# A hybrid decoder block: the recurrence's output projection put ahead of the convolution's

## The chip, the cores and the metric

The kernel runs on one core of a Trainium2 chip, in float32. The metric is the device time of one execution in microseconds (us), as the median of several runs. Three runs of the kernel before gave 1181.91, 1185.55 and 1191.15 us. The engines are named as the profile names them: PE is TensorE's matrix multiply and PEld its weight load, DVE is VectorE, ACT is ScalarE, POOL is GpSimd, SP is SyncE, which here only issues transfers; ACTq and SPq are the queues of two engines.

## The reference

512 tokens of width 1024, with 16 learned tokens ahead of them, go through one layer. What matters here is the mixing half:

```python
p = h @ w_in[l]                                   # one input projection, columns cut into parts
y_conv = conformer_conv(p[..., :c_end], ...)      # GLU, 31-tap conv, LayerNorm over channels, silu, @ w_conv_out
y_rwkv = rwkv7_time_mix(p[..., c_end:r_end], ...) # recurrence over time, norm per head, gate, @ w_rwkv_out
gates = jax.nn.sigmoid(p[..., r_end:] + b_gate[l])
y = gates[..., :D_MODEL] * y_conv + gates[..., D_MODEL:] * y_rwkv
h = layer_norm(ALPHA * h + y @ w_o[l], ln1_g[l], ln1_b[l])
h = layer_norm(ALPHA * h + conv_gated_mlp(h, ffn_up[l], ffn_dw[l], ffn_down[l]), ln2_g[l], ln2_b[l])
```

## The kernel before, in words

Activations lie channels first: 128 channels on the partitions, 514 or 528 tokens along a row, eight such blocks for the width of 1024. Float32 products are made of three passes: every operand is split into a high and a low part (`split`, L136: ACT casts the high part, L138, DVE subtracts it for the low one, L141), and `gemm` (L158) multiplies high by high, low by high and high by low, so that one block of 128 outputs costs two halves of 258 and 256 columns with 8 x 3 matmuls each: 48 in all. `wload` (L155) brings a block of weights from memory (SP, 512 KB), splits it, and holds it in two buffers of each kind, which all products share in turn; so the products follow each other in the order in which the code asks for their weights. Their results go to three PSUM banks (`gbank`).

The code is a long list of steps that SCHEDULE (L50) puts in order. A compiler turns it into one instruction stream for each engine: it takes the steps' place in the list as a priority, and gives an engine that is free the first instruction that is ready. `front()` raises the priority of some of them (weight loads, PSUM reads). A tile whose space is used again waits for the readers of the tile that lay there.

The steps, for block p of eight (two heads of the recurrence each):

- G: the convolution's GLU; T or the second number of S: the convolution, run on DVE between the dependent instructions of a solve; its result is stored to `c_dr` (L725).
- K: three projections; P (`prep`, L347): decays, keys, and the blocks `Gt` of a triangular system.
- S (`solve`, L482): the system's inverse, 31 dependent steps on DVE (L520 to L526, tile `W`), after a trip of `Gt` through memory (`dA`, `L`).
- C (`merge`, L548, and `chain`, L581): the inverse comes back, and nine chunks of the recurrence run one after the other on PE (L584), ACT and DVE.
- F (`finish`, L624): the norm per head, the gate, and a store to `o_dr` (L673).
- A (`gate`, L728): one of 16 blocks of the branch gates, a product from `hhi`, `hlo` with tanh, stored to `g_dr`. A gate depends on nothing but its weights.
- N (`conv_norm`, L745): the eight blocks `c_t` come back from `c_dr`, are normalised over the channels and split into `zh`, `zl`.

After the list come, each over eight blocks: the convolution's projection (L811, operands `zh`, `zl`; result times its gate to `ya_dr`); the loads of `o_dr` into `o_t` with two buffers and their split into `oh`, `ol` (L832); the recurrence's projection (L838; result times its gate, plus `ya`, split into `yh`, `yl`); then the mixing product with `w_o` and the LayerNorm, in two halves of the tokens (L860 to L896), where the first NKEEP blocks of `w_o` are kept in split form for the second half and the others are loaded twice. The feed-forward part follows.

Pools of memory are opened and closed by hand: `scan` (steps S, C, F, A) on the left, `proj` (steps G, K, P, convolution) on the right, later `conv` in the place of `proj`, and `rout` in the place of `scan`. The text says product z for the convolution's projection, product o for the recurrence's, product y for the mixing one, and pair 7 for the last pair of heads with its steps S7, C7 and F7.

Of the kernel before, what the change touches and what calls it, by code (L numbers as in the profile page):

```python
# [42 lines left out]
GN_EPS = 64e-5  # L43
EXPM05 = float(np.exp(-0.5))
BACK = 3000
NKEEP = 6
GW = 132


SCHEDULE = ("G0 K0 P0 T0 G1 S01 K1 P1 C0 K2 F0 G2 S12 K3 P2 C1 G3 F1 K4 S23 G4 P3 C2 F2 A S34 K5 P4 C3 F3 G5 S4 A "  # L50
            "T5 K6 P5 G6 C4 F4 S56 P6 C5 K7 F5 G7 S67 A A A P7 C6 F6 S7 A A C7 A A N A A A A A A A F7")


@with_exitstack
def hybrid_block(ctx: ExitStack, tc: tile.TileContext, a, out, dbg=None):
# [730 lines left out]
    for step in SCHEDULE.split():  # L786
        what, p, q = step[0], int(step[1:2] or 0), int(step[2:] or -1)
        if what == "K":
            raw[p] = rkv(p)
        elif what == "P":  # L790
            prs[p] = prep(p, *raw.pop(p))
        elif what == "S":
            solved[p] = solve(prs[p], conv(q, cpads.pop(q)) if q >= 0 else ())
        elif what == "C":
            with front():
                merge(prs[p], *solved[p])
                ys[p] = chain(prs[p])
        elif what == "F":
            finish(prs[p], ys.pop(p))
        elif what == "G":  # L800
            cpads[p] = glu(p)
        elif what == "T":
            with back():
                for _ in conv(p, cpads.pop(p)):
                    pass
        elif what == "A":
            gate(gates.pop(0))
        elif what == "N":
            ctx_a1.close()
            rb, zh, zl = conv_norm()  # L810
    for j in range(NK):  # L811
        ga = rb.tile([P, NQ], F32, name="ga", bufs=2)
        nc.sync.dma_start(out=ga, in_=g_dr[j])
        w = wload(a["w_conv_out"][0], P * j)
        for sl, n in qsl:
            pt = gbank()
            gemm(pt[:, :n], w, lambda k, s: zh[k][:, s], lambda k, s: zl[k][:, s], sl)
            with front():
                V.scalar_tensor_tensor(out=ga[:, sl], in0=ga[:, sl], scalar=1.0, in1=pt[:, :n],
                                       op0=ALU.add, op1=ALU.mult)  # L820
        nc.sync.dma_start(out=ya_dr[j], in_=ga)
    ctx_b1.close()
    ctx_a2.close()


    ctx_b2, ctx_o = ExitStack(), ExitStack()
    op = pool(ctx_o, "rout", "left")
    mp = pool(ctx_b2, "mix", "right")
    ot = lambda dt, name: op.tile([P, NQ], dt, name=name, tag="ot", bufs=16)
    yt = lambda dt, name: mp.tile([P, NQ], dt, name=name, tag="yt", bufs=16)  # L830
    oh, ol, yh, yl = [], [], [], []
    for j in range(NK):  # L832
        o_t = op.tile([P, NQ], F32, name="o_t", bufs=2)
        nc.sync.dma_start(out=o_t, in_=o_dr[j])
        oh.append(ot(F32R, "oh"))
        ol.append(ot(F32R, "ol"))
        split(oh[j], ol[j], o_t)
    for j in range(NK):  # L838
        gb_ = op.tile([P, NQ], F32, name="gb_", bufs=2)
        nc.sync.dma_start(out=gb_, in_=g_dr[8 + j])  # L840
        ya = op.tile([P, NQ], F32, name="ya", bufs=2)
        nc.sync.dma_start(out=ya, in_=ya_dr[j])
        w = wload(a["w_rwkv_out"][0], P * j)
        yh.append(yt(F32R, "yh"))
        yl.append(yt(F32R, "yl"))
        for sl, n in qsl:
            pt = gbank()
            gemm(pt[:, :n], w, lambda k, s: oh[k][:, s], lambda k, s: ol[k][:, s], sl)
            with front():
                V.scalar_tensor_tensor(out=gb_[:, sl], in0=gb_[:, sl], scalar=1.0, in1=pt[:, :n],  # L850
                                       op0=ALU.add, op1=ALU.mult)
            V.tensor_tensor(out=ya[:, sl], in0=ya[:, sl], in1=gb_[:, sl], op=ALU.add)
            S.activation(out=yh[j][:, sl], in_=ya[:, sl], func=AF.Copy, scale=0.5)
            V.scalar_tensor_tensor(out=yl[j][:, sl], in0=ya[:, sl], scalar=0.5, in1=yh[j][:, sl].bitcast(F32),
                                   op0=ALU.mult, op1=ALU.subtract)


    ctx_o.close()
    h1h, h1l = hhi[:, :, Q0:T], hlo[:, :, Q0:T]
    ctx_f = ExitStack()  # L860
    fw = pool(ctx_f, "upw", "left")
    kept = [wload(a["w_o"][0], P * j, mp, bufs=NKEEP) for j in range(NKEEP)]
    half_tile = lambda name, n, bufs: mp.tile([P, 258], F32, name=name, bufs=bufs)[:, :n]
    for (t0, t1), (sl, n) in zip(QH, qsl):
        pm, pv = abank(), abank()
        xs = []
        s1, s2 = half_tile("s1", n, 1), half_tile("s2", n, 1)
        for j in range(NK):
            w = kept[j] if j < NKEEP else wload(a["w_o"][0], P * j)
            pt = gbank()  # L870
            gemm(pt[:, :n], w, lambda k, s: yh[k][:, s], lambda k, s: yl[k][:, s], sl)
            x1 = half_tile("x1", n, 10)
            with front():
                V.scalar_tensor_tensor(out=x1, in0=hlo[:, j, t0:t1].bitcast(F32), scalar=ALPHA,
                                       in1=pt[:, :n], op0=ALU.mult, op1=ALU.add)
                V.scalar_tensor_tensor(out=x1, in0=hhi[:, j, t0:t1].bitcast(F32), scalar=ALPHA,
                                       in1=x1, op0=ALU.mult, op1=ALU.add)
            xs.append(x1)
            if j > 0:
                V.tensor_tensor(out=s1, in0=xs[0] if j == 1 else s1, in1=x1, op=ALU.add)  # L880
        TE.matmul(pm[:, :n], ones_d, s1, start=True, stop=True)
        with front():
            for j in range(NK):
                V.tensor_tensor(out=xs[j], in0=xs[j], in1=pm[:, :n], op=ALU.subtract)
                sq = s2 if j == 0 else half_tile("xsq", n, 2)
# [4 lines left out]
            rs1 = mp.tile([P, 258], F32, name="rs1")[:, :n]  # L890
            S.activation(out=rs1, in_=pv[:, :n], func=AF.Sqrt, bias=eps_ln)
            V.reciprocal(out=rs1, in_=rs1)
            for j in range(NK):
                V.tensor_tensor(out=xs[j], in0=xs[j], in1=rs1, op=ALU.mult)
                S.activation(out=xs[j], in_=xs[j], func=AF.Identity, scale=par("ln1_g", j), bias=par("ln1_b", j))
                split(h1h[:, j, sl], h1l[:, j, sl], xs[j], "s")  # L896
    dump("h1", h1h.bitcast(F32))


    fl = ExitStack()  # L900
    ctx_b2.close()
    fp = pool(fl, "ffn", "right")
    hidh = fp.tile([P, NF, SEQ], F32R, name="hidh")
# [113 lines left out]
```

## Time and profile before

| | us |
|---|---|
| median of three runs | 1185.55 |
| lowest, highest | 1181.91, 1191.15 |
| the profiled execution, own time | 1188.6 |
| its span in the trace | 1186.6 |
| PE busy in it | 1128.4 (95%) |
| DVE busy in it | 870.5 (73%) |
| ACT busy in it | 560.5 (47%) |

The profile is of one execution. Times in its views count from the span's start. A matmul's busy time is longer than its share of the stream, since matmuls are pipelined; where a rate is wanted, the count of matmuls in a stretch is divided by the stretch. A few matmul records are missing. The granted clock is given as a share of full speed, 2.4 GHz; its lower level, 1.2 GHz, shows as 0.5.

### The profile page before, as it was taken

Reading aid. Unit: us, or ns where it says so; the run is one execution under the profiler, and the core shown is the slowest. Engines: PE = TensorE matmul, PEld = TensorE weight load, DVE = VectorE, ACT = ScalarE, POOL = GpSimd, SP = SyncE. Lnnn points to the kernel's source line nnn. Section 1 sums busy time; section 2 is a strip of 40 time slices with the busy share of each in tenths; the row PEclk is TensorE's granted clock in tenths of the full one; section 3 lists DMA queues with packets and bytes.
Section 4 is the critical chain, followed back from the end, with each engine's and each line's share of the span. In section 5 each row is a group of like instructions: output and inputs, shape, how many; then the busy total and the mean of one; then the engine's idle time right before and its main releaser. Section 6 shows DMA issues by size and latency. Waiting matters only on the chain.

```text
span 1186.6 us, 22669 instructions
## 1 busy us (share of the span) xinstructions
PE 1128.4 (95%) x8718; PEld 1062.5 (90%) x8718; DVE 870.5 (73%) x2195; ACT 560.5 (47%) x1195; POOL 85.0 (7%) x242
## 2 busy tenths in 40 slices
PE   4998999999999999999978989999999999999997
PEld 3997989989898989998978989989999999998885
DVE  8598988989899998986495346688876666652227
ACT  3544355647556565666575433346433443432120
POOL 6001011101101110101000000000000000000000
PEclk9999999999999999999898989999999999999999
DMA  5324241333424143344443376523332323343321
GB/s 159 82 80 106 64 117 41 90 82 89 95 60 108 41 104 84 79 121 108 135 125 85 103 209 193 164 58 85 107 100 80 104 75 107 90 134 98 93 85 71
DMA packets 202439, 118.99 MB, mean 100 GB/s; under 512 B 50036, under 2 KB 186397, under 8 KB 202331
## 3 DMA queue, kind: packets, MB, share of 16 engines
q1 hardware_dynamic: 182992, 113.81, 34.1%
q10 hardware_dynamic: 17515, 3.17, 1.5%
q8 instruction: 68, 1.11, 0.4%
q0 software_dynamic: 1824, 0.57, 0.2%
q14 instruction: 40, 0.33, 0.1%
HBM read 102.24 MB, written 15.28 MB: 99 GB/s over the span
## 4 chain that ended last, share of the span: by engine, by line
PE 60%; DVE 8%; DMA 7%; ACT 3%; issue 2%; ACTq 0%; SPq 0%; DVEq 0%; POOL 0%; POOLq 0%
PE ps_g L161 13%; PE ps_g L162 13%; PE ps_g L163 13%; PE ps_x L584 7%; PE psf L961 3%; PE psf L963 3%; PE psf L962 3%; DMA wr<-in_w_o_dram 2%; DMA t22s<-dT 1%; DMA o_t<-o_dr 1%; DVE wl L141 1%; ACT wh L138 1%; PE ps_a L450 1%; DMA wr<-in_ffn_up_dram 1%; PE ps_m L571 1%
## 5 line engine op out<-in xcount | busy, mean ns | idle before, releaser
L161 PE MATMUL ps_g<-hhi,wh 128*128 128x256 f32 (+2 forms) x1648 | 477.2, 290 | 7.9 <-ACT hf_t L277 3.9
L162 PE MATMUL ps_g<-hhi,wl 128*128 128x256 f32 (+2 forms) x1648 | 477.3, 290 | 0.0
L163 PE MATMUL ps_g<-hlo,wh 128*128 128x256 f32 (+2 forms) x1648 | 474.6, 289 | 0.0
L161 PEld LDWEIGHTS ps_g<-hhi,wh 128*128 128x128 f32 x1648 | 312.8, 190 | 11.3 <-ACT hf_t L277 4.5
L162 PEld LDWEIGHTS ps_g<-hhi,wl 128*128 128x128 f32 x1648 | 312.4, 190 | 2.6 <-issue 0.6
L163 PEld LDWEIGHTS ps_g<-hlo,wh 128*128 128x128 f32 x1648 | 312.9, 190 | 1.3 <-issue 0.4
L141 DVE TENSOR_TENSOR wl<-wr,wh 128x1024 fp32r<-128x1024 f32 x151 | 184.1, 1220 | 96.6 <-ACT wh L138 96.0
L138 ACT CAST wh<-wr 128x1024 fp32r<-128x1024 f32 x151 | 158.0, 1047 | 124.8 <-PE psf L962 75.2
L722 DVE SCALAR_TENSOR_TENSOR cev<-cd,drv,cev 128x257 f32<-128x257 f32 x216 | 99.1, 478 | 0.1
L919 ACT COPY pu<-ps_g 128x258 f32<-128x258 f32 (+1 forms) x88 | 32.8, 373 | 111.1 <-PE ps_g L163 111.0
L584 PE MATMUL ps_x<-UV,Gt 128*66 128x64 f32 (+1 forms) x576 | 71.3, 246 | 4.2 <-DMA Gt<-dT 3.8
L584 PEld LDWEIGHTS ps_x<-UV,Gt 128*66 128x66 f32 (+1 forms) x576 | 65.5, 168 | 6.1 <-DMA Gt<-dT 4.0
L961 PE MATMUL psf<-wh,hidh 128*128 128x512 f32 x176 | 69.3, 394 | 0.0
L963 PE MATMUL psf<-wl,hidh 128*128 128x512 f32 x176 | 69.0, 392 | 0.0
L962 PE MATMUL psf<-wh,hidl 128*128 128x512 f32 x176 | 68.3, 388 | 0.0
L926 DVE SCALAR_TENSOR_TENSOR u<-pu,prm,u 128x512 f32<-128x512 f32 x88 | 65.7, 748 | 1.3
L714 DVE SCALAR_TENSOR_TENSOR csh<-cpad,drv,csh 128x257 f32<-128x257 f32 x120 | 57.5, 479 | 0.5
L615 DVE SCALAR_TENSOR_TENSOR Sb<-Sb,lc,ps_x 64x64 f32<-64x64 f32 x112 | 31.3, 280 | 32.7 <-PE ps_x L584 31.2
L924 DVE TENSOR_SCALAR u<-pu,prm 128x512 f32<-128x512 f32 x44 | 21.2, 485 | 43.5 <-ACT pu L919 43.4
L524 DVE TENSOR_TENSOR stmp<-L,W 128x60 f32<-128x60 f32 (+21 forms) x216 | 45.3, 210 | 1.3
L526 DVE TENSOR_TENSOR W<-W,stmp 128x60 f32<-128x60 f32 (+21 forms) x216 | 45.2, 209 | 1.0
L161 PE MATMUL ps_g<-zh,wh 128*128 128x258 f32 (+1 forms) x128 | 38.5, 303 | 7.6 <-ACT zh L138 7.6
(308 smaller groups left out, 1991.9 us busy)
## 6 DMA issues: line engine op xcount, KB each, us to landing
wr<-in_w_in_dram SPq DMA_DIRECT2D x59, 512.0 KB, 4.3
wr<-in_ffn_up_dram SPq DMA_DIRECT2D x44, 512.0 KB, 4.0
wr<-in_ffn_down_dram SPq DMA_DIRECT2D x22, 512.0 KB, 3.7
wr<-in_w_o_dram SPq DMA_DIRECT2D x10, 512.0 KB, 4.9
g_dr<-gt SPq DMA_DIRECT2D x16, 257.0 KB, 3.0
L<-dA SPq DMA_DIRECT2D x32, 128.0 KB, 4.2
wr<-in_w_conv_out_dram SPq DMA_DIRECT2D x8, 512.0 KB, 4.4
wr<-in_w_rwkv_out_dram SPq DMA_DIRECT2D x8, 512.0 KB, 5.6
```

Of the source, the lines that this page charges most:

```text
L138: S.copy(out=dst_hi, in_=src)
L141: V.tensor_tensor(out=dst_lo, in0=src, in1=dst_hi.bitcast(F32), op=ALU.subtract)
L161: TE.matmul(ps, wh[:, k, :], xh(k, sl), start=(k == 0), stop=False)
L162: TE.matmul(ps, wl[:, k, :], xh(k, sl), start=False, stop=False)
L163: TE.matmul(ps, wh[:, k, :], xl(k, sl), start=False, stop=(k == nk - 1))
L584: mm = lambda o, l, r, start: TE.matmul(o, l, r, start=start, stop=True, skip_group_check=True)
L714: yield V.scalar_tensor_tensor(out=cs_, in0=x1[:, i:i + NM], scalar=dcol(D_SCW, 8 * i + j) if i < HT else dcol(D_HCW, 8 * 2 * i + j), in1= ...
L722: yield V.scalar_tensor_tensor(out=yp[:, b, :] if lasttap else ev[:, b, :], in0=d[:, i:i + NM], scalar=dcol(D_HCW, 8 * (2 * i + b) + j), i ...
L926: V.scalar_tensor_tensor(out=u, in0=p_[:, t:t + SEQ], scalar=pcol(C_FW, 44 * t + m), in1=u, op0=ALU.mult, op1=ALU.add)
L961: TE.matmul(acc[t][d], hidh[:, k, ts], wd[k][0][:, ds], start=(k == 0), stop=False)
L962: TE.matmul(acc[t][d], hidl[:, k, ts], wd[k][0][:, ds], start=False, stop=False)
L963: TE.matmul(acc[t][d], hidh[:, k, ts], wd[k][1][:, ds], start=False, stop=(k == NF - 1))
```

## The change

Four edits. First, the order after the list: the loads and splits of `o_t` and product o come first, `conv_norm` and product z second. What product o gives, times its gate, is stored to `ya_dr` and read back in product z, where the sum, the factor 0.5 and the split into `yh`, `yl` now are. Step N leaves the list. Second, `o_t` has eight buffers instead of two. Third, the list: one gate moves from ahead of P7 and three now stand behind F7; with the others, ten gates stand behind C7 and N is gone. Fourth, NKEEP is 4 instead of 6. Pools move with this: the mixing tiles lie on the left, in the place of `rout`, and the LayerNorm's tiles have a pool of their own, `norm1`, on the right.

```diff
-NKEEP = 6
+NKEEP = 4
-            "T5 K6 P5 G6 C4 F4 S56 P6 C5 K7 F5 G7 S67 A A A P7 C6 F6 S7 A A C7 A A N A A A A A A A F7")
+            "T5 K6 P5 G6 C4 F4 S56 P6 C5 K7 F5 G7 S67 A A P7 C6 F6 S7 A A C7 A A A A A A A F7 A A A")
...
-        elif what == "N":
-            ctx_a1.close()
-            rb, zh, zl = conv_norm()
+
+    ctx_a2.close()
+    ctx_o = ExitStack()
+    op = pool(ctx_o, "rout", "left")
...
     for j in range(NK):
-        ga = rb.tile([P, NQ], F32, name="ga", bufs=2)
+        o_t = op.tile([P, NQ], F32, name="o_t", bufs=NK)
+        nc.sync.dma_start(out=o_t, in_=o_dr[j])
+        oh.append(ot(F32R, "oh"))
+        ol.append(ot(F32R, "ol"))
+        split(oh[j], ol[j], o_t)
+    for j in range(NK):
+        gb_ = op.tile([P, NQ], F32, name="gb_", bufs=2)
+        nc.sync.dma_start(out=gb_, in_=g_dr[8 + j])
+        w = wload(a["w_rwkv_out"][0], P * j)
+        for sl, n in qsl:
+            pt = gbank()
+            gemm(pt[:, :n], w, lambda k, s: oh[k][:, s], lambda k, s: ol[k][:, s], sl)
+            with front():
+                V.scalar_tensor_tensor(out=gb_[:, sl], in0=gb_[:, sl], scalar=1.0, in1=pt[:, :n],
+                                       op0=ALU.add, op1=ALU.mult)
+        nc.sync.dma_start(out=ya_dr[j], in_=gb_)
+    ctx_a1.close()
+    rb, zh, zl = conv_norm()
+    ctx_o.close()
+    ctx_f, ctx_b2 = ExitStack(), ExitStack()
+    fw = pool(ctx_f, "upw", "left")
+    mp = pool(ctx_b2, "mix", "left")
...
+    for j in range(NK):
+        ga = mp.tile([P, NQ], F32, name="ga", bufs=2)
         nc.sync.dma_start(out=ga, in_=g_dr[j])
+        ya = mp.tile([P, NQ], F32, name="ya", bufs=2)
+        nc.sync.dma_start(out=ya, in_=ya_dr[j])
         w = wload(a["w_conv_out"][0], P * j)
+        yh.append(yt(F32R, "yh"))
+        yl.append(yt(F32R, "yl"))
...
-        nc.sync.dma_start(out=ya_dr[j], in_=ga)
-    ctx_b1.close()
-    ctx_a2.close()
...
-        o_t = op.tile([P, NQ], F32, name="o_t", bufs=2)
...
-            V.tensor_tensor(out=ya[:, sl], in0=ya[:, sl], in1=gb_[:, sl], op=ALU.add)
+            V.tensor_tensor(out=ya[:, sl], in0=ya[:, sl], in1=ga[:, sl], op=ALU.add)
...
+    ctx_b1.close()
...
+    ctx_n = ExitStack()
+    lnp = pool(ctx_n, "norm1", "right")
     kept = [wload(a["w_o"][0], P * j, mp, bufs=NKEEP) for j in range(NKEEP)]
-    half_tile = lambda name, n, bufs: mp.tile([P, 258], F32, name=name, bufs=bufs)[:, :n]
+    half_tile = lambda name, n, bufs: lnp.tile([P, 258], F32, name=name, bufs=bufs)[:, :n]
...
+    ctx_n.close()
     ctx_b2.close()
```

## Rows read from the trace of the kernel before

**Rows 1.** Windows: stretch, length, busy PE, PEld, DVE, ACT, POOL (instructions), clock, DMA, GB/s.
```profile
614.64:638.16 23.52, 12.90 (x73) 11.95 (x73) 19.42 (x48) 15.10 (x23) 0.29 (x1) 0.71 0.21 50
638.16:693.73 55.57, 55.57 (x470) 53.35 (x470) 23.05 (x55) 22.53 (x53) 0.00 (x0) 1.00 0.51 157
693.73:707.29 13.56, 10.15 (x56) 9.08 (x54) 4.51 (x8) 3.98 (x7) 0.00 (x0) 0.75 0.71 197
707.29:747.42 40.13, 40.09 (x330) 39.88 (x331) 27.08 (x52) 14.88 (x24) 0.00 (x0) 1.00 0.58 171
747.42:799.52 52.10, 48.66 (x392) 47.49 (x391) 42.80 (x92) 20.67 (x37) 0.00 (x0) 1.00 0.35 102
```

**Rows 2.** Waits of PE, 540 to 820 us: line, for whom, total, times, longest.
```profile
PE ps_g L161 <- ACT zh L138: 7.6, 1, 7.6
PE ps_g L161 <- ACT oh L138: 2.9, 3, 1.5
```

**Rows 3.** Timeline of PE: C6's end, last gate matmul, C7's first and last chunk.
```profile
593.66 0.66 PE L584 MATMUL ps_x<-UV,Gt 128*128 128x64 f32 x4
...
614.36 0.28 PE L163 MATMUL ps_g<-hlo,wh 128*128 128x256 f32 x1
...
642.25 0.40 PE L584 MATMUL ps_x<-UV,Gt 128*66 128x64 f32 x4
...
666.43 0.64 PE L584 MATMUL ps_x<-UV,Gt 128*128 128x64 f32 x4
```

**Rows 4.** Timeline of SP: transfers issued, with time and the issue's length.
```profile
569.22 0.45 SPq L752 DMA_DIRECT2D c_t<-c_dr  x1
570.49 1.24 SPq L502 DMA_DIRECT2D L<-dA  x3
580.50 0.40 SPq L147 DMA_DIRECT2D wr<-in_w_in_dram  x1
580.94 0.58 SPq L502 DMA_DIRECT2D L<-dA  x1
...
677.75 0.38 SPq L673 DMA_DIRECT2D o_dr<-on  x1
...
680.99 0.90 SPq L834 DMA_DIRECT2D o_t<-o_dr  x2
```

**Rows 5.** Timeline of DVE: S7's first and last steps.
```profile
588.45 0.82 DVE L520 SCALAR_TENSOR_TENSOR W<-L,W 128x31 f32<-128x31 f32 x3
...
630.96 0.17 DVE L526 TENSOR_TENSOR W<-W,stmp 128x8 f32<-128x8 f32 x1
```

**Rows 6.** Windows of two tiles (length, DVE busy): first `c_t` with ACT, then `W` with POOL.
```profile
588.45:631.13 42.68, 19.87 (x36) 11.74 (x19) 0.87 0.34 107
...
588.45:631.13 42.68, 12.59 (x58) 0.00 (x0) 0.87 0.34 107
```

**Rows 7.** Groups of DVE instructions in that stretch: busy us, mean ns, idle before.
```profile
L141 DVE TENSOR_TENSOR wl<-wr,wh 128x1024 fp32r<-128x1024 f32 x4 | 4.9, 1218 | 0.0
L769 DVE TENSOR_TENSOR qsum<-qsum,csq 128x514 f32<-128x514 f32 x7 | 4.8, 690 | 0.0
...
L774 DVE RECIPROCAL rstd<-rstd 128x258 f32<-128x258 f32 (+1 forms) x2 | 3.5, 1749 | 0.0
```

**Rows 8.** Timeline of ACT: the first casts of `o_t`.
```profile
686.31 1.33 ACT L138 CAST oh<-o_t 128x514 fp32r<-128x514 f32 x2 [2.81 <-DMA o_t<-o_dr]
```

**Rows 9.** Chain that ended last, pieces of C6: start, length, what.
```profile
570.63 1.17 PE ps_x L584 x6
...
574.37 0.73 PE ps_x L584 x6
...
577.52 0.70 PE ps_x L584 x6
```

**Rows 10.** Windows, columns as in rows 1: a stretch of C6, one of product o.
```profile
566.00:574.00 8.00, 8.00 (x54) 7.55 (x53) 4.62 (x18) 3.86 (x13) 0.00 (x0) 0.63 0.47 107
698.00:706.00 8.00, 6.53 (x34) 6.35 (x33) 2.08 (x3) 1.24 (x2) 0.00 (x0) 0.57 0.86 245
```

**Rows 11.** Transfers: what, queue, count, size, median us from issue to landing.
```profile
o_dr<-on SPq DMA_DIRECT2D x8, 257.0 KB, 3.0
...
o_t<-o_dr SPq DMA_DIRECT2D x8, 257.0 KB, 5.1
```

More of the change, by code (lines that the diff above doesn't have):

```diff
@@ L807, in hybrid_block @@
             gate(gates.pop(0))
-        elif what == "N":
-            ctx_a1.close()
-            rb, zh, zl = conv_norm()
-    for j in range(NK):
-        ga = rb.tile([P, NQ], F32, name="ga", bufs=2)
[L813 to L820, printed above, removed]
-        nc.sync.dma_start(out=ya_dr[j], in_=ga)
-    ctx_b1.close()
-    ctx_a2.close()
[L826 to L832, printed above, removed]
-        o_t = op.tile([P, NQ], F32, name="o_t", bufs=2)
+    ctx_a2.close()
+    ctx_o = ExitStack()
+    op = pool(ctx_o, "rout", "left")
+    ot = lambda dt, name: op.tile([P, NQ], dt, name=name, tag="ot", bufs=16)
+    oh, ol = [], []
+    for j in range(NK):
+        o_t = op.tile([P, NQ], F32, name="o_t", bufs=NK)
         nc.sync.dma_start(out=o_t, in_=o_dr[j])
@@ L840, in hybrid_block @@
         nc.sync.dma_start(out=gb_, in_=g_dr[8 + j])
-        ya = op.tile([P, NQ], F32, name="ya", bufs=2)
-        nc.sync.dma_start(out=ya, in_=ya_dr[j])
         w = wload(a["w_rwkv_out"][0], P * j)
-        yh.append(yt(F32R, "yh"))
-        yl.append(yt(F32R, "yl"))
         for sl, n in qsl:
@@ L851, in hybrid_block @@
                                        op0=ALU.add, op1=ALU.mult)
-            V.tensor_tensor(out=ya[:, sl], in0=ya[:, sl], in1=gb_[:, sl], op=ALU.add)
+        nc.sync.dma_start(out=ya_dr[j], in_=gb_)
[5 more added lines that the diff above has]
+    mp = pool(ctx_b2, "mix", "left")
+    yt = lambda dt, name: mp.tile([P, NQ], dt, name=name, tag="yt", bufs=16)
+    yh, yl = [], []
+    for j in range(NK):
+        ga = mp.tile([P, NQ], F32, name="ga", bufs=2)
+        nc.sync.dma_start(out=ga, in_=g_dr[j])
+        ya = mp.tile([P, NQ], F32, name="ya", bufs=2)
+        nc.sync.dma_start(out=ya, in_=ya_dr[j])
+        w = wload(a["w_conv_out"][0], P * j)
+        yh.append(yt(F32R, "yh"))
+        yl.append(yt(F32R, "yl"))
+        for sl, n in qsl:
+            pt = gbank()
+            gemm(pt[:, :n], w, lambda k, s: zh[k][:, s], lambda k, s: zl[k][:, s], sl)
+            with front():
+                V.scalar_tensor_tensor(out=ga[:, sl], in0=ga[:, sl], scalar=1.0, in1=pt[:, :n],
+                                       op0=ALU.add, op1=ALU.mult)
+            V.tensor_tensor(out=ya[:, sl], in0=ya[:, sl], in1=ga[:, sl], op=ALU.add)
             S.activation(out=yh[j][:, sl], in_=ya[:, sl], func=AF.Copy, scale=0.5)
@@ L855, in hybrid_block @@
                                    op0=ALU.mult, op1=ALU.subtract)
-    ctx_o.close()
+    ctx_b1.close()
     h1h, h1l = hhi[:, :, Q0:T], hlo[:, :, Q0:T]
-    ctx_f = ExitStack()
-    fw = pool(ctx_f, "upw", "left")
+    ctx_n = ExitStack()
+    lnp = pool(ctx_n, "norm1", "right")
     kept = [wload(a["w_o"][0], P * j, mp, bufs=NKEEP) for j in range(NKEEP)]
-    half_tile = lambda name, n, bufs: mp.tile([P, 258], F32, name=name, bufs=bufs)[:, :n]
+    half_tile = lambda name, n, bufs: lnp.tile([P, 258], F32, name=name, bufs=bufs)[:, :n]
     for (t0, t1), (sl, n) in zip(QH, qsl):
@@ L889, in hybrid_block @@
             TE.matmul(pv[:, :n], ones_d, s2, start=True, stop=True)
-            rs1 = mp.tile([P, 258], F32, name="rs1")[:, :n]
+            rs1 = lnp.tile([P, 258], F32, name="rs1")[:, :n]
             S.activation(out=rs1, in_=pv[:, :n], func=AF.Sqrt, bias=eps_ln)
```

## The prediction

> **What bounds the kernel now.** I read the page first: PE is busy 1128.4 us of a span of 1186.6, so the question is where PE is not streaming. Then the windows around the places that the diff moves. There the time between the last gate and the mixing product (614.6 to 747.4 us) falls into four stretches [rows 1]. In the first, 23.5 us, PE has run out of gates (the last matmul of a gate starts at 614.36 [rows 3]) and waits for the first `zh` [rows 2], at a granted clock of 0.71. In the second, 55.6 us, PE is never idle: product z runs between the chunks of C7 and the matmuls of F7. In the third, 13.6 us, product o starts and stops while `o_t` arrives in two buffers. The fourth is product o at full speed, 330 matmuls in 40.13 us, which is 0.1216 us for each; a product of 384 is 46.7 us.
>
> So of the first and third stretch (37.1 us) only 129 matmuls, 15.7 us, are work; about 21 us stand idle or half clocked. That is what the change can win at most by filling.
>
> The second view is what pair 7 waits for. S7's steps on DVE run from 588.45 to 631.13 [rows 5], though its 58 instructions are 12.6 us of work [rows 6]. Between them DVE does the convolution's norm: 36 instructions on `c_t` (19.9 us [rows 6]), the sum of squares (4.8) and the reciprocals (3.5) [rows 7], 28.2 us in all. From the last step to the store of the last block of o (677.75 [rows 4]) it is another 46.8 us: the inverse's trip, C7 (642.25 to 667.07 [rows 3]) and F7, 10.7 us. That latency costs nothing before, since product z covers it.
>
> **The change part by part.**
>
> *Order of the products.* Product o needs all eight blocks of o, as its sum runs over all channels; so it can't be finished for any output before F7 has stored. Behind it in the queue of weights stands product z: both take their weights through the same two buffers in the code's order, so product z, though its operands are ready, can't pass ahead. PE then has, between the last gate and F7's store, only C7 and F7 themselves. Their own work follows from the second stretch, 470 instructions in 55.57 us: of the 73 matmuls of the first stretch some 60 are product z's (the others are the norm's and the merge's), so 324 of its 384 are left for the second, 39.4 us, and 16 us are pair 7's. The cover of product z is gone for a stretch that lasts from 614.6 to past 677.75.
>
> *Gates put last.* Their place in the list is a priority and not a time. Before, the last nine gates stand behind C7 in the list, and PE has done them 28 us before C7's first chunk [rows 3], because it was free. The change moves one gate and adds none. Whatever the order, PE has the same work before product o, so this edit moves neither C7's start nor product o: 0 us. It would be worth something only if gates were missing as cover earlier; there PE is busy to 614.36.
>
> *The norm of the convolution, moved behind product o.* Does S7 become quicker? The loads of `c_t` are the test. In the list N stands behind C7, yet the first `c_t` was issued at 569.22 [rows 4], 73 us ahead of C7's first chunk: a load goes out when its place is free and SP has nothing better. Its place is `proj`'s, free at the same time after the change; nothing in the change delays it but its priority. So I take it that the norm still runs between S7's steps: S7 unchanged, bounds 0 and a gain of 23 us (42.7 less 12.6, less 4.9 for four weight splits [rows 7], less some 2 for F6). I take 0, as the row shows the very same jump ahead.
>
> *C7 without cover.* With PE idle around it the granted clock falls, as it did in the first stretch. C6 shows a chunk at either clock: 3.74 us (570.63 to 574.37) where the clock was 0.63 [rows 9, 10], 3.15 us for the next, at full clock. Eight chunks cost 0 to 8 x 0.6 = 4.7 us; I take 4.7, as PE will be emptier than there. F7's store is issued at 682.4.
>
> *Eight buffers.* All `o_t` loads can be issued at once, 0.4 us each. Before, the first was issued 3.2 us after F7's store and its cast began 5.3 us later [rows 4, 8]. After, first operand ready: 682.4 + 0.4 + 5.3 + 0.6 = 688.7. The last waits for the store to land (3.0 [rows 11]), then for its load, cast and subtraction: 682.4 + 3.0 + 5.3 + 0.6 + 0.7 = 692.0. Meanwhile three banks can take seven eighths of their matmuls, 63, 7.7 us. Product o therefore counts as started between 688.7 and 692; I take 690.4, 8 us behind the store. The first matmuls run at the lower clock: 34 in 8 us before in such a place, where 66 fit [rows 10], 3.9 us lost, part of it waits; I take 3, bounds 0 and 3.9.
>
> *Products o and z* then run unbroken: 768 x 0.1216 = 93.4 us. The norm is long done. Reading `ya` back and the mixing sums have 5.8 us a block to hide in, as they had before.
>
> *Four kept weights.* Two more blocks of `w_o` are loaded and split in the mixing stage: two casts on ACT, which is free there, and 2 x 1.22 us on DVE, busy 42.8 of 52.1 us [rows 1]. Bounds 0 and 2.4; I take 1.5.
>
> *Sum.* 690.4 + 3 + 93.4 = 786.8 for the start of product y, against 747.4: +39.4, and 1.5 more: +40.9. What follows is unchanged. The profiled execution took 1188.6 us, 3 us over the median; on the median of 1185.55 the forecast is 1226.5, rounded to 1226. With the bounds of its own costs it is 1214 to 1238.
>
> A rule that speaks against the change: the Trainium skill, "Perfetto Trace Analysis", section Optimization Strategy, advises to interleave stretches that have different limits. The stretch from 638.16 is such an interleaving, a chain of latency and a product, with PE never idle [rows 1]. By the rule the change should cost what the cover was worth; that is the sum above, got from rows alone.
>
> **The rivals.**
>
> *S7 freed* (chance 0.25). The norm's loads do wait their turn behind `o_t`, since everything ahead of them on SP has the higher priority. Then S7 ends 23 us earlier, near 608, and the norm hides under product o, 46.7 us against its 28.2 on DVE. Against it speaks the jump of `c_t` in [rows 4]. Gates and C7 then overlap a little; the store comes at 657.7, product y at 762.1: +14.7 and 1.5, so 1202. S7 may also start earlier: the fourth load of `L` was issued 9.2 us after the other three, behind a weight load [rows 4]. Without this it is 1193.
>
> *C7 early enough to be covered by gates* (chance 0.07), the other side. If S7 were over when C6 ends (594.3 [rows 3]), C7 could follow at once: 594.3 + 24.8 + 10.7 = 629.8 for the store, 8 more for the loads, 93.4 for the products: 731.2. That is 16.2 earlier, less 1.5: 1171. It decides at a store before 641.5, which means S7's last step before 594.7. Before, S7 began at 588.45 and has 12.6 us of dependent work, so it would have to begin seven microseconds earlier and run alone; only the delayed load of `L` leaves room for that.
>
> *Only the two stalls go*: the 21 us of the first and third stretch won and nothing lost, 1165. It needs product o ready at some 631, when PE has done gates, C7 and F7 back to back; the line above shows that the chain alone can't. No chance of its own.
>
> **How the numbers follow.** Unchanged S7 has 0.68, S7 freed 0.25, C7 covered 0.07. One per cent, 12 us, is about what a measurement of this kernel can tell from no change. The first is slower throughout; of the second, about half (1193 to 1197) lies within 1%; the third is mostly faster. So faster 0.06, same 0.14, slower 0.80. The range of 1192 to 1238 leaves out the third case and the edges of the others, some 0.15.
>
> **What would show it.** In the profile after: PE's windows nearly empty from some 615 to 690 us but for C7, with a clock near 0.5; `c_t` loads still near 570 to 585; S7's last step near 631; F7's store near 680; eight `o_t` loads in one burst behind it; product o and product z back to back with no wait; product y's first matmul near 787. If the `c_t` loads stand behind the `o_t` loads, the first rival holds. The forecast is wrong altogether if product z's matmuls appear ahead of product o's end, or if F7's store comes before 642.

## The result, and the profile after

The changed kernel takes 1216.74 us (median of four runs, 1213.43 to 1221.16) beside 1186.79 for the kernel before on the same chip: a ratio of 1.026, 95% interval 1.0224 to 1.0297. It is slower, as forecast, and inside the range; but it is 9 us faster than the forecast of 1226, and the trace shows that one step of the sum was wrong by 18 us and three others by 3 to 6 us, not all in the same direction.

The profiled execution took 1221.16 us (span 1219.5), the slowest of the four. It was already 4.45 us behind when S7 began (592.90 against 588.45 [rows 5]) and 3 us behind at 331 us, in code that is, but for one gate, the same in both. The granted clock was lower there: 0.97 instead of 0.99 from 100 to 335 us, and 0.88 instead of 0.91 from 550 us to S7's first step, together some 10 us more at its lower level. So positions are compared below as distances from S7's first step.

Windows of the kernel after (stretch, length, busy PE, PEld, DVE, ACT, POOL with instructions, clock, DMA, GB/s), cut at the last gate's end, product o's first matmul, product z's last, product y's first and its end:

```profile
618.67:678.85 60.18, 35.55 (x161) 28.67 (x160) 33.45 (x76) 34.15 (x75) 0.00 (x0) 0.57 0.15 33
678.85:728.95 50.10, 49.97 (x386) 49.26 (x387) 20.23 (x30) 11.69 (x14) 0.00 (x0) 0.93 0.59 184
728.95:775.28 46.33, 46.33 (x384) 46.28 (x384) 27.45 (x53) 15.57 (x24) 0.00 (x0) 1.00 0.63 189
775.28:825.79 50.51, 47.87 (x390) 47.19 (x389) 41.59 (x86) 20.54 (x35) 0.00 (x0) 1.00 0.41 115
```

The picture that the prediction drew is there: where before a stretch of 23.5 us and one of 13.6 were poorly filled [rows 1], now one of 60 us is, at a granted clock of 0.57, with 161 matmul instructions; then o and z run back to back. The timeline of SP shows the norm's loads jumping ahead, as predicted, and the eight `o_t` loads in one burst behind F7's store:

```profile
573.85 0.39 SPq L752 DMA_DIRECT2D c_t<-c_dr  x1
...
586.48 2.76 SPq L752 DMA_DIRECT2D c_t<-c_dr  x5
...
674.34 0.34 SPq L673 DMA_DIRECT2D o_dr<-on  x1
674.72 4.03 SPq L816 DMA_DIRECT2D o_t<-o_dr  x8
```

But the store comes 81.4 us after S7's first step; before it was 89.3, and the prediction had 93.9. The timeline of DVE shows why: S7's steps take 24.8 us instead of 42.7 [rows 5].

```profile
592.90 1.11 DVE L520 SCALAR_TENSOR_TENSOR W<-L,W 128x31 f32<-128x31 f32 x4
...
617.53 0.18 DVE L526 TENSOR_TENSOR W<-W,stmp 128x8 f32<-128x8 f32 x1
619.14 1.43 DVE L764 TENSOR_TENSOR c_t<-c_t,ps_a 128x258 f32<-128x258 f32 x4 [1.43 <-PE ps_a L762]
...
627.44 3.09 DVE L769 TENSOR_TENSOR qsum<-qsum,csq 128x514 f32<-128x514 f32 x4 [0.52 <-ACT csq L767]
632.59 0.57 DVE L615 SCALAR_TENSOR_TENSOR Sb<-Sb,lc,ps_x 64x64 f32<-64x64 f32 x2 [2.05 <-PE ps_x L584]
633.19 2.30 DVE L769 TENSOR_TENSOR qsum<-qsum,csq 128x514 f32<-128x514 f32 x3
636.74 0.59 DVE L615 SCALAR_TENSOR_TENSOR Sb<-Sb,lc,ps_x 64x64 f32<-64x64 f32 x2 [1.25 <-PE ps_x L584]
```

The seven sums of `c_t` (L755, L757) still run between S7's steps; everything from the first subtraction on (L764) comes after them, and now runs between C7's chunks. The subtraction waited for a product of PE, L762, the mean over the channels. The timeline of PE after has it directly behind the last gate:

```profile
618.39 0.28 PE L163 MATMUL ps_g<-hlo,wh 128*128 128x256 f32 x1
618.51 1.03 PE L762 MATMUL ps_a<-csum,ones_d 128*128 128x258 f32 x4
624.01 1.92 PE L566 MATMUL ps_m<-t11n,a 128*128 128x32 f32 x8 [4.48 <-DVE t11n L561]
...
628.97 0.71 PE L584 MATMUL ps_x<-UV,Gt 128*66 128x64 f32 x4 [0.78 <-ACT Gt L572]
...
663.60 1.12 PE L584 MATMUL ps_x<-UV,Gt 128*128 128x64 f32 x4 [0.35 <-ACT UV L606]
```

and the timeline of PE before has it in the midst of the gates, which ran to 614.36 [rows 3]:

```profile
597.79 1.14 PE L762 MATMUL ps_a<-csum,ones_d 128*128 128x258 f32 x4
```

Step N stood ahead of seven gates in the list; it now stands behind all of them. TensorE's stream is put together by that priority, and a gate is always ready. So a norm of 28 us on DVE stood still for one small product. In C7, from the first chunk's first matmul to the last one's, the time is 34.6 us where it was 24.2 [rows 3].

### The profile page after: what moved, and what is told of

It is laid out like the page before. It is cut to its first block, busy times and chain, and to the rows that moved or that the text cites. A ratio compares the mean times of both kernels' runs of the same rounds, so it can differ in the third digit from the quotient of the medians.

```text
span 1219.5 us, 22690 instructions
## 1 busy us (share of the span) xinstructions
PE 1146.3 (94%) x8718; PEld 1076.8 (88%) x8718; DVE 877.8 (72%) x2197; ACT 563.9 (46%) x1197; POOL 85.0 (7%) x242
## 4 chain that ended last, share of the span: by engine, by line
PE 63%; DVE 7%; DMA 4%; ACT 4%; issue 2%; POOL 0%; ACTq 0%; SPq 0%; DVEq 0%; POOLq 0%
PE ps_g L162 14%; PE ps_g L161 14%; PE ps_g L163 14%; PE ps_x L584 8%; PE psf L968 3%; PE psf L970 3%; PE psf L969 3%; PE ps_a L450 1%; DMA t22s<-dT 1%; DMA t<-dT 1%; DVE wl L141 1%; PE ps_m L571 1%; DMA dT<-W 1%; ACT wh L138 1%; DVE W L526 1%
## 5 line engine op out<-in xcount | busy, mean ns | idle before, releaser
L584 PE MATMUL ps_x<-UV,Gt 128*66 128x64 f32 (+1 forms) x576 | 76.2, 258 | 6.0 <-DMA Gt<-dT 3.9
L584 PEld LDWEIGHTS ps_x<-UV,Gt 128*66 128x66 f32 (+1 forms) x576 | 70.8, 180 | 8.4 <-DMA Gt<-dT 4.1
L615 DVE SCALAR_TENSOR_TENSOR Sb<-Sb,lc,ps_x 64x64 f32<-64x64 f32 x112 | 31.3, 279 | 27.2 <-PE ps_x L584 25.7
L161 PE MATMUL ps_g<-oh,wh 128*128 128x258 f32 (+1 forms) x128 | 37.8, 296 | 5.2 <-ACT oh L138 5.0
```

The source lines that it names most:

```text
L161: TE.matmul(ps, wh[:, k, :], xh(k, sl), start=(k == 0), stop=False)
L584: mm = lambda o, l, r, start: TE.matmul(o, l, r, start=start, stop=True, skip_group_check=True)
```

## Experiments

Theory: the time after is (a) a chain S7, C7, F7 that nothing covers, (b) shortened by 18 us because the norm's product stands behind the gates, (c) lengthened by some 10 us in C7, by the half clock and by the norm that now runs beside it, (d) 5 us in the mixing stage for the kept weights. The main rival: S7 and C7 would be the same wherever the norm's product stands, and the difference is the clock alone. All times are medians; the ratio is to the kernel before on the same chip.

| kernel | us | ratio (95% interval) |
|---|---|---|
| changed kernel | 1216.74 | 1.026 (1.0224 to 1.0297) |
| norm early | 1226.91 | 1.0364 (1.0332 to 1.0395) |
| gates held | 1237.34 | 1.0442 (1.0406 to 1.0478) |
| norm late | 1234.23 | 1.0432 (1.0384 to 1.048) |
| norm late, its products in front | 1211.31 | 1.0227 (1.018 to 1.0274) |
| clock kept up | 1203.91 | 1.0172 (1.0126 to 1.0219) |
| norm late, in front, clock kept up | 1212.51 | 1.0225 (1.0182 to 1.0269) |
| two buffers | 1220.16 | 1.0304 (1.0274 to 1.0334) |
| all but the order | 1189.31 | 1.0035 (1.0013 to 1.0057) |
| four kept weights alone | 1189.30 | 1.0043 (1.0017 to 1.0068) |
| before, clock kept up | 1188.55 | 1.0036 (1.0008 to 1.0064) |
| before, norm first | 1191.50 | 1.0058 (1.0038 to 1.0077) |
| before, norm first, stores on POOL | 1186.41 | 1.0026 (1.0007 to 1.0044) |

What their timelines show, in us. The chunk is the mean distance of C7's state updates on DVE (L615).

| kernel | S7's steps | C7 chunk | S7's start to F7's store | store to first of o | first of o to first of y |
|---|---|---|---|---|---|
| before | 42.7 | 3.25 | 89.3 | 16.0 | 53.7 |
| changed | 24.8 | 4.56 | 81.4 | 4.5 | 96.4 |
| norm early | 42.7 | 4.16 | 95.1 | 4.3 | 96.0 |
| gates held | 44.0 | 3.10 | 94.2 | 14.2 | 94.7 |
| norm late | 19.9 | 4.17 | 77.0 | 7.3 | 118.6 |
| late, in front | 20.0 | 4.17 | 77.5 | 7.3 | 96.4 |
| clock kept up | 24.8 | 3.65 | 74.4 | 4.9 | 93.6 |
| late, in front, clock | 19.6 | 3.09 | 68.4 | 11.5 | 98.2 |
| two buffers | 24.8 | 4.56 | 81.3 | 5.0 | 100.3 |

**The norm's place in the list.** The changed kernel with the norm's step back where it was, ahead of the last gates:

```diff
- "... S7 A A C7 A A A A A A A F7 A A A"     # conv_norm() behind product o
+ "... S7 A A C7 A A N A A A A A F7 A A A"
```

> Kernel after with the convolution's norm put back into the list behind C7 and two gates, as before; product o still first. Theory (S7 was quicker after because the norm's first product, L762, had to wait behind the gates on PE, so that the rest of the norm left DVE alone until S7 was over): S7's last step moves from 617.7 back to about 630, C7's chunks get quicker (3.2 to 3.7 us instead of 4.5) since the norm is over by then, F7's store is 3 to 8 us later: 1219 to 1225. Rival (the norm's place has nothing to do with S7): S7's last step stays near 618, 1217.

Measured: 1226.91 us, 10 us over the changed kernel, a little above what was expected. Its timeline of PE has L762 early again, and the merge of C7 (L566) waiting long for S7:

```profile
593.47 1.14 PE L762 MATMUL ps_a<-csum,ones_d 128*128 128x258 f32 x4
...
633.02 1.92 PE L566 MATMUL ps_m<-t11n,a 128*128 128x32 f32 x8 [19.75 <-DVE t11n L561]
```

S7 is back at 42.7 us. This kernel is the one that the prediction had worked out: the store 95.1 us behind S7's start (93.9 in the sum), 1226.9 us (1226). That the sum comes out so closely is in part luck: in this kernel C7 takes about 7 us more than before where 4.7 were taken, and the stage from product y on 5 us more instead of 1.5, while product o and z come to product y 4 us sooner behind the store than was taken. The place of one step in a list, with its loads as early as ever, is worth 10 us.

**Gates held back.** The same from the other side: the changed kernel, where gates 11 to 15 come behind C7's merge on TensorE, so that they cover C7:

```diff
- gemm(pt[:, :n], w, hh, hl, slice(t0, t1))
+ gemm(pt[:, :n], w, hh, hl, slice(t0, t1), held=merged[7] if j >= HELD else None)   # HELD = 11
...
```

> The changed kernel with one edit: the matmuls of gates 11 to 15 wait on TensorE for the merge of C7 (pair 7), so that five gates, some 29 us of matmuls, run beside C7's chunks instead of ahead of them. The work is the same. Theory (cover by gates is worth what TensorE loses between the last gate and product o; TensorE works for 29 us less before C7 and 29 us more beside it): chunks at full clock, 3.4 to 3.6 us, so F7's store 7 to 8 us earlier, product o no later for the gates, time 1207 to 1211 us against 1217. First rival (the gates are what the norm waits for, as its first product stood behind them): the norm comes earlier by up to 29 us, delays S7 as in the run with the norm early, time 1217 to 1227. Second rival: the gates are not done when o is ready, product o is as late as before, time 1215 to 1219.

Measured: 1237.34 us, worse than every case expected; the first rival's mechanism is what happened, and the second's with it. Its timeline of PE and its windows:

```profile
603.08 2.08 PE L767 MATMUL ps_a<-csum,ones_d 128*128 128x258 f32 x4 [2.74 <-DVE csum L762]
```

```profile
590.00:620.00 30.00, 18.30 (x73) 13.94 (x73) 22.96 (x86) 14.25 (x37) 0.90 (x2) 0.50 0.02 9
620.00:640.00 20.00, 4.00 (x12) 2.96 (x12) 15.45 (x38) 11.45 (x20) 0.00 (x0) 0.50 0.13 20
```

With no gates ahead of it the norm's product (L767 here) comes as soon as `csum` is there, and S7 takes 44.0 us. C7's chunks do get their full clock (3.10), but the store is at 94.2, and the held gates bring product o's first matmul 14.2 us behind the store. Gates were not worth more as cover for C7 than where they stood: as cover they win 1.1 us a chunk (3.10 against 4.16 in the kernel with the norm early, where the norm is over by then too), while their absence ahead of the norm gave it its way in S7.

**The norm late.** Its loads behind F7's last store, so that it runs under product o:

```diff
- nc.sync.dma_start(out=c_t, in_=c_dr[j])
+ behind(nc.sync.dma_start(out=c_t, in_=c_dr[j]), stored[-1], "norm behind the last o")
...
```

> The changed kernel with one edit: the loads of c_t are issued behind the last store of F7, so that nothing of the convolution's norm runs beside S7 or C7; it runs under product o. Theory (what is left of the norm delays S7's steps and C7's chunks by queueing on DVE): S7's steps take 20 to 22 us instead of 24.8, a chunk of C7 4.1 to 4.2 us instead of 4.56, F7's store comes 5 to 7 us earlier, product z follows product o without a wait, time 1209 to 1213 us against the changed kernel's 1217. Rival (the norm only fills DVE's gaps): S7 and the chunks as they were, time within 2 us of 1217. Second rival: the norm, 28 us on DVE, is not done under product o and product z starts late, time above 1217.

Measured: 1234.23 us: the second rival, 17 us over the changed kernel. What the theory said of S7 and C7 nearly holds (19.9, 4.17, the store 4.4 us nearer, where 5 to 7 were expected), but three loads of `c_t` now go out ahead of those of `o_t`, so that product o starts 7.3 us behind the store instead of 4.5, and then product z waits. The timeline of PE (with one row of DVE first, the last sums of `c_t`):

```profile
680.22 1.42 DVE L759 TENSOR_TENSOR csum<-csum,c_t 128x514 f32<-128x514 f32 x2
```

```profile
717.11 0.28 PE L163 MATMUL ps_g<-ol,wh 128*128 128x256 f32 x1
717.23 1.03 PE L764 MATMUL ps_a<-csum,ones_d 128*128 128x258 f32 x4
729.86 2.08 PE L774 MATMUL ps_a<-qsum,ones_d 128*128 128x258 f32 x4 [11.60 <-DVE qsum L771]
```

`csum` is ready at 681.64; its product (L764 here) comes at 717.23, behind the last matmul of product o. It is the same small product as before, standing this time behind 384 matmuls. So the norm, 28 us, began when product o was over.

**The norm late, its two products in front.** The same, and:

```diff
+ with front():
      TE.matmul(pm[:, :n], ones_d, csum[:, sl], start=True, stop=True)   # and the same for qsum
```

> The changed kernel with the norm's loads behind the last store of F7, as in the run with the norm late, and besides that the norm's two small products (csum and qsum with the matrix of ones) at the scan's priority, so that TensorE takes them between product o's matmuls and not behind all of them. Theory (the 17 us that the late norm lost were its two products standing behind product o in TensorE's order; what it gained, 8 us from S7's first step to F7's store, is real): product z follows product o with no wait over 2 us, time 1208 to 1213 us against the changed kernel's 1217 and 1234 with the norm late. Rival (the norm is too long for product o, 28 us on DVE beside o's own 17): z waits 5 us or more, time 1215 to 1225.

Measured: 1211.31 us, as the theory had it: 23 us less than with the norm late, by the place of two products. Product z follows o without a wait (96.4 us for both). Against the changed kernel it is 5 us better by the medians, though the two intervals overlap; product y comes 1.2 us nearer to S7's first step, and 3.4 us nearer to C6's first chunk.

**The clock.** In the changed kernel C7 and product o's beginning run at half clock for most of their time. 288 unused matmuls of the lowest priority, ahead of product o, keep TensorE at work:

```diff
+ with back():
+     for g in range(12):
+         pt = gbank()
+         for k in range(24):
+             TE.matmul(pt[:, :258], hhi[:, k % NK, 0:P], hhi[:, (k + 1) % NK, Q0:Q0 + 258], start=(k == 0), stop=(k == 23))
```

> The changed kernel with 288 matmuls more (128 x 258, float32r) at the lowest priority, ahead of product o in the program, whose results nobody uses: they are no part of the computation and only keep TensorE at work while C7 runs. Theory (of the 4.56 us of a C7 chunk some 1.0 us is TensorE's half clock, and product o's first matmuls run at half clock for some 3 us): granted clock between 620 and 680 us near 1.0 instead of 0.5 to 0.7, chunks 3.5 us, product o 47 us instead of 49.9, time 1205 to 1209 us against 1217. Rival (the chunk is slow because of DVE and ACT): clock up, chunks 4.4 us or more, time 1214 to 1217. Second rival: the added matmuls stand in the way of C7's own, time above 1217.

Measured: 1203.91 us, 13 us less by the medians and 10 us by the two ratios, which were taken on different chips: within the range of the theory or slightly better. Windows of the changed kernel, then of this one:

```profile
620.00:640.00 20.00, 12.75 (x56) 10.66 (x56) 12.83 (x30) 10.15 (x23) 0.00 (x0) 0.60 0.23 54
640.00:660.00 20.00, 14.08 (x74) 11.85 (x73) 14.45 (x28) 12.41 (x27) 0.00 (x0) 0.59 0.00 1
```

```profile
620.00:640.00 20.00, 20.00 (x178) 18.98 (x177) 15.18 (x30) 11.75 (x29) 0.00 (x0) 1.00 0.00 1
640.00:660.00 20.00, 19.77 (x171) 19.26 (x171) 8.59 (x25) 14.65 (x32) 0.00 (x0) 1.00 0.08 21
```

The granted clock is 1.00 where it was 0.60 (between its two levels of 1.2 and 2.4 GHz), a chunk takes 3.65 us instead of 4.56, and o and z together 93.6 instead of 96.4: 7.1 us to the store and 2.8 in product o, 10 us together. The Trainium skill, "TensorE: Matmul & The Clock Gate", section Why this matters for your kernels, advises against idle gaps between bursts of matmuls, as the clock falls in them; this pair of runs agrees, and gives the price here.

**Both together.** The late norm with its products in front, and the 288 unused matmuls:

> The kernel of the run before (norm under product o, its products at the scan's priority) with the 288 unused matmuls of the run with the clock kept up; they are no part of the computation. Theory (norm and clock are separate prices of the turned order, 5 to 8 us and 13 us): both come off, time 1195 to 1202 us, so that 10 to 17 us over the kernel before stay as the plain price of the uncovered chain. Rival (with TensorE at full clock the norm no longer slows the chunks, or the unused matmuls stand in the way): no better than 1204.

Measured: 1212.51 us: the rival. The two gains are there up to F7's store, 68.4 us behind S7's start, the shortest of all; a chunk of 3.09 us with neither the norm beside it nor the half clock completes a square: 4.56 with both, 4.17 with the half clock alone, 3.65 with the norm alone (the square is not quite even, as the granted clock was 0.60 in the first and 0.50 in the second). But then product o starts 11.5 us behind the store. The first of `oh` is cast from 660.62 on ACT, and TensorE is still at the unused matmuls (L817):

```profile
660.62 5.37 ACT L138 CAST oh<-o_t 128x514 fp32r<-128x514 f32 x8 [8.10 <-DMA o_t<-o_dr]
```

```profile
663.76 2.12 PE L817 MATMUL ps_g<-hhi 128*128 128x258 f32 x17
665.72 0.28 PE L161 MATMUL ps_g<-oh,wh 128*128 128x258 f32 x1
```

So 4 us were lost to filling that stood in the way (11.5 us against 7.3 without it); another 23 of the 288 came as late as 720 and 802 us. What a fitting amount of it would give wasn't tried.

**Two buffers, and what the small edits cost.** The changed kernel with two `o_t` buffers:

> Kernel after with two o_t buffers instead of eight. Theory: the loads go out in pairs, each pair after the split of the one before, four trips of 5.3 us and a split instead of one burst; product o's effective start 8 to 14 us later, 1225 to 1231. Rival: product o can use the first blocks while the others come, so that less than 4 us are lost, under 1221.

Measured: 1220.16 us, 3.4 more: the buffers were worth less than expected. The two intervals overlap, but the trace agrees: product o and z take 100.3 us instead of 96.4. Everything but the order, that is the kernel before with the gate moved, eight buffers and four kept weights:

> Kernel before with every part of the change but the order: one gate moved from ahead of P7 to the end of the list, eight o_t buffers, four kept blocks of w_o; product z still first. Theory (the loss is product z's cover of C7 and F7): product y starts near 741 instead of 747, since the third stretch loses its waits, the mixing stage is 1.5 to 3 us longer; time 1180 to 1186 against 1187. Rival (the list or the four kept blocks carry much of the 30 us): over 1195.

Measured: 1189.31 us, above the expected range and 4 us over the kernel before beside it: nothing is gained. The order alone is thus worth 27 us. Its timeline of SP shows why eight buffers do little there: the loads are spread over 11 us, between product z's transfers (683 to 694 us).

```profile
679.57 0.38 SPq L673 DMA_DIRECT2D o_dr<-on  x1
...
682.21 0.90 SPq L834 DMA_DIRECT2D o_t<-o_dr  x2
...
685.08 1.70 SPq L834 DMA_DIRECT2D o_t<-o_dr  x2
...
690.22 0.90 SPq L834 DMA_DIRECT2D o_t<-o_dr  x2
...
692.80 0.44 SPq L834 DMA_DIRECT2D o_t<-o_dr  x1
```

And the kernel before with `NKEEP = 4` alone:

> Kernel before with four kept blocks of w_o instead of six, nothing else. Theory: two more loads and splits in a stage where DVE is busy 43 of 52 us cost 1.5 to 3 us: 1188 to 1190. Rival: the stage has room for them, 1187.

Measured: 1189.30 us, in the expected range, but only because the kernel before ran at 1184.97 beside it: the cost is 4 to 5 us (interval 0.17 to 0.68%), more than the 1.5 to 3 of the theory. Product y itself takes no longer (50.8 us from its first matmul to its last, 52.1 before). But the wait for the LayerNorm's split output ahead of the feed-forward part is longer, and the granted clock falls there. The wait before, then the same in this kernel and in the changed one:

```profile
PE ps_g L161 <- ACT hhi L138: 1.7, 1, 1.7
...
PE ps_g L161 <- ACT hhi L138: 4.2, 1, 4.2
```

Windows of 12 us, each from 64.7 us behind product y's first matmul, before and after:

```profile
812.00:824.00 12.00, 10.25 (x86) 10.00 (x86) 10.25 (x23) 9.69 (x22) 0.00 (x0) 1.00 0.00 1
...
840.00:852.00 12.00, 7.25 (x41) 6.76 (x42) 8.93 (x20) 7.40 (x20) 0.00 (x0) 0.72 0.00 0
```

In the same 12 us TensorE starts 41 matmuls instead of 86.

**Can the kernel before be bettered with this?** Three tries, none better. First, unused matmuls in its two stalls, six groups of 24 ahead of product z and two of 18 ahead of product o:

> The kernel before with 180 unused matmuls at the lowest priority, no part of the computation: six groups of 24 ahead of product z, two of 18 ahead of product o. Theory (in the stalls of the kernel before, too, the clock that falls costs time: product z's first 11 us at 0.89, 1.2 us, and product o's first 8 us at 0.57 with 34 matmuls where 66 fit, 3.9 us): time 1180 to 1184 us against 1186, ratio 0.995 to 0.998. Rival (TensorE's order is fixed, so unused matmuls that are not over when zh or oh is ready delay the product): 1186 to 1192.

Measured: 1188.55 us, the rival. Windows of the stretches of [rows 1], the first and the third:

```profile
614.64:638.16 23.52, 23.25 (x194) 22.65 (x192) 18.88 (x47) 15.98 (x26) 0.00 (x0) 1.00 0.22 52
...
693.73:707.29 13.56, 13.34 (x110) 12.95 (x109) 7.07 (x13) 5.23 (x8) 0.00 (x0) 1.00 0.79 234
```

TensorE is never idle and never slow, and product y starts at 747.21, where it started at 747.42: product o ran in 47 us instead of 54, but began 5.4 us later, behind the filling; 17 of the 180 did not come ahead of a product at all but in the mixing stage, from 786 us on. A busy share is not progress.

Second, the norm ahead of S7 in the list of the kernel before:

```diff
- "... P7 C6 F6 S7 A A C7 A A N A A A A A A A F7"
+ "... P7 C6 F6 N S7 A A C7 A A A A A A A A A F7"
```

> The kernel before with one edit in its list: N stands ahead of S7 instead of seven gates behind C7, so the norm of the convolution goes first on DVE and in TensorE's order, and S7's steps take what it leaves. The work is the same. Theory (norm and S7 share DVE for 43 us and only their order is free; whichever goes first sets which product starts): product z starts near 620 instead of 639.7 and covers all of S7's tail, C7 and F7; F7's store as before near 677, since norm and S7 together end near 631 as before; product o then starts when its loads are in, near 688 to 690 instead of 693.7, at half clock; time 1180 to 1184 us against 1186, ratio 0.995 to 0.999. Rival (S7 behind the norm ends later than 631, and product z's matmuls stand ahead of C7's on TensorE): F7's store at 684 or later, time 1186 to 1195.

Measured: 1191.50 us, the rival. The theory's first term was misread: the 639.7 given there for the kernel before is not product z's start, whose first matmul is at 625.21; with the norm first it is at 624.02, so there was next to nothing to win. S7 starts later and ends at 631 as before, and F7's store comes 8.3 us later than before, at 686.08; product o starts at 693.10, as before, and takes 2 us longer. Why C7 is late although S7 is not, the timeline of SP shows:

```profile
631.37 1.21 SPq L544 DMA_DIRECT2D dT<-W  x2
637.82 0.33 SPq L821 DMA_DIRECT2D ya_dr<-ga  x1
638.32 0.38 SPq L553 DMA_DIRECT2D t<-dT  x1
...
643.03 0.39 SPq L147 DMA_DIRECT2D wr<-in_w_conv_out_dram  x1
643.46 0.58 SPq L557 DMA_DIRECT2D Gt<-dT  x1
```

The read of the inverse, `t<-dT`, stands behind the store of product z's first result, which waits for that product; in the kernel before it was issued 3 us behind `dT`'s stores. And the last read of `Gt` stands behind a weight load that waits for its buffer. So third, the same with product z's gate loads and result stores issued by POOL:

```diff
-         nc.sync.dma_start(out=ga, in_=g_dr[j])
+         nc.gpsimd.dma_start(out=ga, in_=g_dr[j])        # and the same for ya_dr
```

> The kernel with the norm first, and besides that product z's gate loads (ga) and result stores (ya_dr from ga) are issued by POOL instead of SP. With the norm first, the read of dT that C7 needs was issued at 638.32 us, right behind the store of product z's first result at 637.82, 7 us behind dT's own stores; in the kernel before it was issued at 634.21, 3 us behind them. Theory (the 8 us by which C7's first chunk came later with the norm first are SP's fixed order, a store that waits for a product standing ahead of the chain's load): the read of dT is issued near 634.5, C7's first chunk 3 to 6 us earlier, F7's store near 680 to 682, product o from 688 to 690, time 1184 to 1188 us against 1191.5 with the norm first; with all 8 us back 1182. Rival (the read waits for the landing of dT's stores, which product z's weight transfers slow): no change, 1190 to 1193.

Measured: 1186.41 us, 5 us less and within the theory's range, but on another chip; over the kernel before by 0.26% (0.07 to 0.44) where the norm first was over it by 0.58% (0.38 to 0.77), so that 4 us are left, and the intervals overlap a little. Its timeline of SP:

```profile
628.70 1.22 SPq L544 DMA_DIRECT2D dT<-W  x2
633.50 0.38 SPq L553 DMA_DIRECT2D t<-dT  x1
...
639.76 0.39 SPq L147 DMA_DIRECT2D wr<-in_w_conv_out_dram  x1
640.19 0.90 SPq L557 DMA_DIRECT2D Gt<-dT  x1
```

The read comes 4.8 us behind the stores instead of 7; `Gt` still stands behind the weight load. That one wasn't moved. The trace shows less than the time does: counted from S7's last step, C7's first state update comes 1.8 us sooner than with the norm first (of the 8 that it was late), F7's store 1.0 us and product y 2.0 us. The other differences between the two profiles lie ahead of S7's end (2.7 us) and behind product y's start (4.0 us), and nothing ties them to the edit. So the theory's mechanism is there, at a quarter of its size; most of the 8 us stays unexplained, and the weight load ahead of `Gt` is a candidate that was not tried. The Trainium skill, "DMA: Bandwidth & Descriptors", section Issuing engines are not separate DMA queues, says that issuing from another engine saves only the time of the issue. Here an issue on SP is 0.3 to 0.4 us, and the read came 2.2 us sooner, so what moving them saved was more than that time: the waiting behind a store on a queue that keeps its order.

## Why the prediction was right or wrong

Slower, and in the range: right. By its own steps, as distances from S7's first step, profile against profile:

| step | predicted | measured |
|---|---|---|
| S7's steps | 0 | -17.9 |
| S7's end to C7 | 0 | +0.1 |
| C7, first to last chunk | +4.7 | +10.5 |
| C7's end to F7's store | 0 | -0.6 |
| store to product y (69.7 before) | +34.7 | +31.3 |
| mixing stage and what follows | +1.5 | +5.0 |
| sum | +40.9 | +28.4 |

28.4 and the 4.45 us by which this execution was late are the 32.8 us between the spans. The sums of the prediction come out as written, with two exceptions that change nothing: the first stretch holds 68 matmuls of product z and not some 60, and the bounds of its own costs, S7 left out, add up to 1216 to 1230, where 1214 to 1238 is written.

*Order of the products: right.* Product o could not start before F7's store, product z did not pass it, o and z ran back to back, and the cover was gone for the whole stretch. It is 27 us of the 30 (all but the order: 1189.31).

*The norm, "S7 unchanged": the step that failed.* "The loads of `c_t` are the test" took the loads for the work. They jumped ahead just as forecast, at 573.85, and the sums with them; but the next instruction of the norm is TensorE's, and TensorE was busy with gates. The rival "S7 freed", at 0.25, had the effect (18 us of its 23) by the wrong queue: it looked for the loads behind `o_t` on SP. Its 1193 to 1202 were not reached: it had S7 5 us shorter than it became and 50 us from there to the store, where 57 were measured, most of it in C7. That the place of the norm's product is the cause is shown by the two kernels that bring it forward (42.7 and 44.0 us of S7).

*"Gates put last: 0 us": right for the gates, blind to the norm.* The gates' own time did not change, as argued (in the kernel with all but the order, the store is 89.4 us behind S7's first step, 89.3 before). But with N gone from among them all gates stand ahead of the norm's product, and that is worth the 10 us by which the kernel with the norm early is slower.

*C7 without cover: right mechanism, half the size.* It was 10.5 us and not 4.7, and the bound of 4.7 was too low. The 4.7 us came from a chunk of C6 at a clock of 0.63, in the midst of other work; at 0.5 throughout, the clock costs 1.08 us a chunk (4.17 against 3.09) and the norm beside it 0.39 (4.56 against 4.17); before, a chunk took 3.25.

*Start of product o: 3.5 us too much.* The first matmul came 4.5 us behind the store, and o and z took 3 us more than 93.4, as said; 8 + 3 had been taken.

*Four kept weights: mis-sized.* 1.5 us, bounds 0 to 2.4; 5.0 in the trace, and 5 us alone in the kernel before. The bounds priced the splits. What the time shows instead is a longer wait for the LayerNorm of the second half (4.2 us instead of 1.7) and the granted clock at 0.72 around it instead of 1.00; that it is the two more splits on DVE which delay the LayerNorm is argued and not shown.

*Eight buffers* are worth 3 to 4 us in the new order, and nothing that shows in the old one. There the trace has product o 2 us shorter with them (51.9 us to product y, 53.7 before), but with two buffers and four kept weights it is 51.7 as well, and the two kernels take the same time (1189.31 and 1189.30).

So the 12.5 us between 40.9 and 28.4 are mainly -17.9 and -3.4 against +5.8 and +3.5; that the forecast missed the median by no more than 9 us is luck, since the errors were of opposite sign. What stays open: how much of the gates' cover a better amount of unused matmuls would buy back, and why C7 starts 6 us late with the norm first and the stores on POOL.

## What to carry to other kernels

Before you say that a moved step "still runs early", follow its chain across engines to the first instruction on a queue that keeps its order, and see what stands ahead of it there: here one small product behind the gates held a norm of 28 us, once to advantage (10 us) and once to harm (23 us), and a 0.3 us store held up a load by some 2 us. When a chain of latency loses its cover, price every term at the clock that TensorE was granted where it idles, and count the work that will move in beside it. Filling that only keeps an engine busy must be over when the real operand is ready, or it takes back what the clock gave.

## What the runs showed of the hardware

- At half clock (0.50 for 40 us) a chunk of C7 is only 1.08 us longer than at full clock (4.17 against 3.09). If what runs on TensorE takes twice as long at half clock, that is a third of a chunk; the other two thirds, by this estimate, are the hops between TensorE, ACT and DVE.
- Between 620 and 660 us, with C7's own matmuls and no filling, the granted clock was 0.59 to 0.60 with the norm's work beside it and 0.50 without; with the unused matmuls it was 1.00.
- The same instructions up to S7 took up to 10 us more or less from one execution to another, and the granted clock went with it. S7's first step is at 583.24, 586.78 and 592.90 in three kernels with the same code up to there (clock kept up, two buffers, changed); from 550 us to that step the clock was 1.00, 0.91 and 0.88, and from 100 to 335 us it was 0.99, 0.99 and 0.97. The runs of the kernel before go the same way: the shortest, 1178.10 us, had a mean clock of 0.990, the longest, 1191.57, one of 0.979. Distances within one trace are the safer measure.
